# A Conformer encoder in float32r on one core: one weights tile with two offsets, casts in program order, and x sums moved by 96 bytes

## The chip, the cores and the metric

One NeuronCore of a Trainium2 chip runs the whole program. The metric is the device time of one execution in microseconds (us); lower is better. Before the change it is 1783.02 us, the median of 3 runs (1781.78 to 1783.49). Engines are named as in the profile: PE (TensorE), PEld (its weight loads), DVE (VectorE), ACT (ScalarE), POOL (GpSimd), SP (SyncE, which issues most loads).

## The reference

Two layers over 512 tokens of width 1024, with feed-forward width 2816:

```python
for l in range(DEPTH):                                   # 2
    x = x + 0.5 * swiglu(rms_norm(x, g1), gate1, up1, down1)
    p = rms_norm(x, gm) @ w_in                           # q and kv latents, rotary key, conv input
    x = x + concat(attention(p), conv(p)) @ w_out        # 8 heads, chunk mask; depthwise conv of 31 taps
    x = x + 0.5 * swiglu(rms_norm(x, g2), gate2, up2, down2)
    x = rms_norm(x, gp)
def swiglu(x, w_gate, w_up, w_down):
    return (silu(x @ w_gate) * (x @ w_up)) @ w_down
```

## The kernel before

x stays in the core's memory, features on partitions and tokens along the free axis. Every large product is made of float32r pieces: an operand is split into a high part `hi` (a cast to float32r on ACT) and a low part `lo = src - hi` (a subtraction on DVE), and `mm3` issues three matmuls on PE, hi by hi (L172), hi by lo (L173) and lo by hi (L174). The right-hand operand is the moving one, the weights the stationary one.

Four kinds of products fill PE:

- **Plain products**, 512 tokens at a time: `group` and `plain` call `mm3` with weights from `load_w`. This is all of the mixing stage (mix), the first two of eleven column pairs of each feed-forward net (FFN), and the last three pairs' down product. In `latent_k`, `queries` and `up_kv` the weights move and the activations are stationary, 288, 384 or 512 columns wide.
- **Strassen products** (`pair` and `down`), 256 columns at a time, called "b11", "t2", "t1", "b22" and so on: `product` issues 2 halves x 4 blocks x 3 = 24 matmuls from `split_into` weights. In the "b22" product half of the moving operands are the `xs` tiles and half are ring tiles; in the others all are ring tiles (`r`).
- **Joined products** ("b21", "t3", "t4"; `product_joined`, L391 and L392): 8 times a 512-column matmul on an `xj` tile (256 tokens of hi beside 256 of lo) and then a 256-column one. The low weights of "b21" and "t4" are in `ls` tiles.
- Attention, in float32, on ring tiles, `q`, `kn` and `m` tiles.

Weights arrive by SP in `raw` or `fr` tiles. `load_w` (L150), `split_into` (L262, L264) and `summed` (L415) take the next of four `wh` buffers for hi and of four `wl` buffers for lo. The scheduler orders the instructions of each engine; `issue_after` fixes some of them by hand.

Where the tiles start within a partition, in bytes modulo 1024, follows from the sizes of what is allocated ahead of them (and from three gaps: `gap`, `gap0`, `gap1`):

| tile | before | after |
|---|---|---|
| ring `r` | 704 | 704 |
| `wh` / `wl` of `load_w` (plain products) | 768 / 896 | 704 / 704 |
| `wh` / `wl` of `split_into`, `summed` (Strassen, joined) | 768 / 896 | 768 / 896 |
| `xs` (x sums of products that are not joined) | 800 | 704 |
| `xj`, `ls`, `fr`, `e`, `u` | 800 | 800 |
| `m`, `y`, `q`, `kn`, `pr` of the mixing stage | 800 | 704 |

A 128-column block of weights is 512 bytes, so a stationary operand starts at its tile's place or 512 bytes on.

Of the kernel before, what the change touches and what calls it, by code (L numbers as in the profile page):

```python
# [7 lines left out]
FP = mybir.dt.float32  # L8
FR = mybir.dt.float32r
# [3 lines left out]
ALU = mybir.AluOpType  # L13
AX = mybir.AxisListType

P = 128
D = 1024
S = 512
# [13 lines left out]
NF = F // P  # L32
EPS = 1e-6
WC = 1024
GAP = 96
HS = S // 2
RING = 35
WIDE = 6
# [11 lines left out]
POOLW = "wo"  # L50
# [29 lines left out]
def encoder_kernel(ctx: ExitStack, tc: tile.TileContext, xT, consts, vecs, rgain, wgu1, wd1, wdq1,  # L80
# [6 lines left out]
    wpool = ctx.enter_context(tc.tile_pool(name="w", bufs=4))  # L87
# [4 lines left out]
    def nm(s):  # L92
        uid[0] += 1
        return f"{s}{uid[0]}"
# [21 lines left out]

    small.tile([P, GAP], FP, tag="gap", name="gap", bufs=1)
    V, A, G, T = nc.vector, nc.scalar, nc.gpsimd, nc.tensor
# [30 lines left out]
    def load_w(src, w, kind=""):  # L149
        raw = wpool.tile([P, WC], FP, tag="raw", name=nm("raw"), bufs=3)  # L150
        nc.sync.dma_start(out=raw[:, :w], in_=src)
        hi = wpool.tile([P, WC], FR, tag="wh", name=nm("wh"))
        order["cast"] = A.copy(hi[:, :w], raw[:, :w]).ins  # L153
        lo = low()
        if kind == "sum":
            A.activation(lo[:, :w], raw[:, :w], AF.Copy, scale=-1.0)
            G.dma_start(out=lo[:, :w], in_=src, accum_op=ALU.add)
            return hi, lo
        (G if kind in POOLW.split() else V).tensor_tensor(lo[:, :w], raw[:, :w], hi[:, :w].bitcast(FP),  # L159
                                                          ALU.subtract)  # L160
        return hi, lo

    def low():
        return wpool.tile([P, WC], FR, tag="wl", name=nm("wl"))

    order = {}

# [82 lines left out]
    def groups(srcs, rhs, ws=None):  # L250

        ws = ws or [load_w(src, WC) for src in srcs]
        os = [bank() for _ in srcs]
        for ks in (range(KD - 1), range(KD - 1, KD)):
            for o, w in zip(os, ws):
                group(o, w, rhs, ks, KD)
        return os

    def split_into(q, src, w=WC):

        hi = wpool.tile([P, WC], FR, tag="wh", name=nm("wh"))
        A.copy(hi[:, :w], src[:, :w])  # L262
        lo = low()
        order["lo"] = V.tensor_tensor(lo[:, :w], src[:, :w], hi[:, :w].bitcast(FP), ALU.subtract).ins  # L264
        return hi, lo

    def ffn(l, gx, norm, wgu, wd, wdq, gain, done, w0=None, halved=KD):
# [3 lines left out]
    def ffn_body(fpool, l, gx, norm, wgu, wd, wdq, gain, done, w0, halved):  # L271
# [2 lines left out]

        def quarter():
            return fpool.tile([P, WC], FP, tag="fr", name=nm("fr"), bufs=4)
# [124 lines left out]
        def subtracted(w, src, n=WC):  # L404

            lo = fpool.tile([P, WC], FR, tag="ls", name=nm("ls"), bufs=2)
            A.activation(lo[:, :n], src[:, :n], AF.Copy, scale=-1.0)  # L407
            G.dma_start(out=lo[:, :n], in_=w, accum_op=ALU.add)  # L408
            return lo

        def summed(w, src, n=WC, lo=None):

            lo = subtracted(w, src, n) if lo is None else lo
            hi = wpool.tile([P, WC], FR, tag="wh", name=nm("wh"))
            A.copy(hi[:, :n], src[:, :n])  # L415
            return hi, lo

        def pair(p, quartered):

            a11, a12, a21, a22, s3 = quarters(wgu[l, p], WC, p == CHUNKS[0][1])  # L420
            bx, by, bz = bank(), (bank(), bank()), (bank(), bank())
            product(bx, split_into("a11", a11), "b11", True, True)
            a = copied(tmp(), bx)
            product_joined(by, summed(wgu[l, p, 1], a12), "b21", True)
            with after("first"):
                V.tensor_tensor(s3, a11, a21, ALU.add)
# [4 lines left out]
            for c, main, rest in parts(by):  # L431
                V.tensor_tensor(a[:, c], a[:, c], main, ALU.add)
                V.tensor_tensor(a[:, c], a[:, c], rest, ALU.add)
                if c.start == 0:
                    A.activation(s[:, 0:HS], a[:, 0:HS], AF.Silu)
            V.tensor_tensor(s[:, 0:HS], s[:, 0:HS], a[:, HS:S], ALU.mult)
            product(bx, split_into("s2", a11), "t2", False, True)
            r2 = wide(fpool.tile([P, WC], FP, tag="e", name=nm("e"), bufs=1))
            copied(r2[:, 0], bx)
            product_joined(bz, split_into("s3", s3), "t3", True)  # L440
            d = [copied(tmp(), o) for o in bz]
            for t in d:
# [3 lines left out]
            for t, (c, _, _) in zip(d, parts(bz)):  # L446
                order["first"] = V.tensor_tensor(r2[:, 1, c], t[:, 0:HS], r2[:, 1, c], ALU.subtract).ins
            product_joined(bz, summed(wgu[l, p, 3], a22), "t4", False)
            for c, main, rest in parts(bz):
                V.tensor_tensor(r2[:, 0, c], main, r2[:, 0, c], ALU.subtract)  # L450
# [28 lines left out]
        def down(act, chunk):  # L479

            n = 2 * NP * P
            for g in range(2):
# [3 lines left out]
                def times(o, src, name, start, q=None, lo=None):  # L486
                    hi, lo = split_into(name, src, n) if q is None else summed(wdq[l, g, chunk, q], src, n, lo)
                    with tc.issue_after(order["pe"]):
                        for k in range(NP):
                            for i in range(2):  # L490
                                c = slice((i * NP + k) * P, (i * NP + k + 1) * P)
                                last = mm3(o[:, i * HS:(i + 1) * HS], hi[:, c], lo[:, c], *act[k][name],
                                           start and k == 0 and i == 0, k == NP - 1, True)
                    order["pe"] = last
# [45 lines left out]
        for p0, p1 in CHUNKS:  # L540
# [3 lines left out]
            for p in range(p0, p1):  # L544
                if p == 0:
                    os = []
                    for r in range(2):
                        ws = w0[2 * r:2 * r + 2] if w0 else [load_w(wgu[l, p, 2 * r + q], WC) for q in range(2)]
                        os.append([bank(), bank()])
                        if w0 and not r:  # L550
                            plain_first(os[r], ws)
                        elif w0:
                            plain(os[r][:1], ws, range(KD))
                            plain([None] + os[r][1:], ws, range(KD // 2))
                            with tc.issue_after(order["mm"]):
                                norm()
                            with after("sums"):
                                plain([None] + os[r][1:], ws, range(KD // 2, KD))
                        else:
                            plain(os[r], ws, range(KD - 1))  # L560
                            plain(os[r], ws, range(KD - 1, KD))
                            if not w0:
                                R = norm()
                    if not w0:
                        scaled(os, R)
                elif p < CHUNKS[0][1]:
                    for r in range(2):
                        ws = [load_w(wgu[l, p, 2 * r + q], WC) for q in range(2)]
                        o = [bank(), bank()]
                        if w0 and not r:  # L570
                            with tc.issue_after(order["mm"]):
                                plain(o[:1], ws, KS[:KD // 4])
                            with tc.issue_after(order["mm"]):
                                R = norm()
                            with after("spread"):
                                plain(o[:1], ws, KS[KD // 4:])
                                plain([None] + o[1:], ws, range(KD))
                            scaled(os, R)
                        else:
                            plain(o, ws, range(KD))  # L580
                        advance(8)
                        act.append(plain_out(o, R))
                else:
                    order.setdefault("pe", order["mm"])
                    act += pair(p, p0 > 0 and not last)
# [9 lines left out]
            for m in range(halved if last else KD):  # L595
                if m in ahead:
                    pd, w = ahead[m]
# [440 lines left out]
    class Finish:  # L1038
# [37 lines left out]
        def part(self, h, src, first):  # L1076
            for t in range(2):
                i = T.matmul(self.ss[:, 2 * h + t:2 * h + t + 1], src[:, t * P:(t + 1) * P], ones[:, 0:1],
                             start=first and h == 0 and t == 0, stop=not first, skip_group_check=True)
            return i.ins  # L1080
# [26 lines left out]
    st = Stats()  # L1107
    f = gained(0, "g1", gx, first_gain)
    f(0)
    w0 = [tuple(wpool.tile([P, w], t, tag=tag, name=nm(tag), bufs=n) for t, tag, n, w in (  # L1110
        (FP, "raw", 3, WC), (FP, "gap0", 1, 16), (FR, "wh", 4, WC), (FP, "gap1", 1, 32), (FR, "wl", 4, WC)))[::2]
        for _ in range(2)]

    def half_w(q, gu):
        raw, hi, lo = (v[:, gu * 512:(gu + 1) * 512] for v in w0[q])
        nc.sync.dma_start(out=raw, in_=wgu1[0, 0, q, :, gu * 512:(gu + 1) * 512])
        A.copy(hi, raw)  # L1117
        V.tensor_tensor(lo, raw, hi.bitcast(FP), ALU.subtract)
    for m in KS:
        if m:  # L1120
            nc.sync.dma_start(out=x[:, m, :], in_=xT[m])
# [6 lines left out]
    w0 = [w[1:] for w in w0]  # L1128
# [172 lines left out]
```

## Time and profile before

| | |
|---|---|
| time, median of 3 runs | 1783.02 us |
| the profiled execution's own time | 1781.53 us |
| its span, first to last instruction | 1779.8 us |
| PE busy | 1768.6 us, 99% of the span |
| PEld / DVE / ACT / POOL busy | 88% / 83% / 62% / 22% |
| mean granted TensorE clock | 0.999 |

Matmuls overlap in the pipeline, so a matmul's own duration is longer than the time from its start to the next one's start. That time, here called the spacing, is what a stream of matmuls costs. It is read from windows of the trace: the length of a stretch without stalls, divided by the matmuls that start in it. Numbers of the trace are counted from the start of the span.

### The profile page before, as it was taken

What the parts mean: (1) busy time and instruction counts of PE and PEld (TensorE: products, weight loads), DVE (VectorE), ACT (ScalarE), POOL (GpSimd) and SP (SyncE); (2) the same over time, 40 slices, a digit from 0 to 9 for tenths busy, and PEclk for the clock granted to TensorE, in tenths of its full rate; (3) what the DMA queues carried; (4) which work ended last, traced back from release to release, by engine and by line L of the source; (5) the groups of instructions that cost most, each with busy time, mean ns of one, the idle gap of its engine ahead of it and who ended that gap; (6) DMA issues with size and microseconds to landing.
All of it is one profiled execution on the core that took longest, in us unless ns stands there. A gap on an engine that the chain in (4) does not pass through costs nothing.

```text
span 1779.8 us, 29441 instructions
## 1 busy us (share of the span) xinstructions
PE 1768.6 (99%) x11430; PEld 1558.0 (88%) x11430; DVE 1486.0 (83%) x2309; ACT 1094.9 (62%) x1699; POOL 383.3 (22%) x315
## 2 busy tenths in 40 slices
PE   9999999999999999999999999999999999999998
PEld 7899999888678899999888999998976788999997
DVE  7998988588965989998779989876989559999883
ACT  5576766456953575757645757554768435757664
POOL 1000000247822000000310000002576410000002
PEclk9999999999999999999999999999999999999999
DMA  5657574324203466665426575743260125575742
GB/s 170 165 140 186 136 189 114 109 86 124 71 25 101 124 162 162 159 166 131 123 66 167 125 197 124 198 112 112 80 157 24 58 68 155 150 180 140 186 117 74
DMA packets 71947, 228.28 MB, mean 128 GB/s; under 512 B 8448, under 2 KB 9600, under 8 KB 71808
## 3 DMA queue, kind: packets, MB, share of 16 engines
q1 hardware_dynamic: 55536, 171.87, 30.5%
q0 software_dynamic: 16128, 54.53, 18.3%
q8 instruction: 89, 1.46, 0.3%
q14 instruction: 50, 0.41, 0.1%
q10 hardware_dynamic: 144, 0.00, 0.0%
HBM read 222.19 MB, written 2.10 MB: 126 GB/s over the span
## 4 chain that ended last, share of the span: by engine, by line
PE 91%; DVE 5%; ACT 2%; issue 1%; DMA 1%; SPq 0%; ACTq 0%; DVEq 0%
PE ps L172 24%; PE ps L174 24%; PE ps L173 23%; PE ps L391 11%; PE ps L392 6%; DVE cv L972 1%; PE ps L921 1%; DVE mx L880 1%; PE ps L899 1%; DVE wl L264 1%; PE ps L876 0%; PE ps L678 0%; PE ps L216 0%; PE ps L914 0%; DVE r L902 0%
## 5 line engine op out<-in xcount | busy, mean ns | idle before, releaser
L172 PE MATMUL ps<-r,wh 128*128 128x256 f32 (+1 forms) x2556 | 808.8, 320 | 1.7 <-ACT wh L1117 0.6
L173 PE MATMUL ps<-r,wh 128*128 128x256 f32 (+1 forms) x2556 | 807.4, 316 | 0.8 <-DVE r L180 0.4
L174 PE MATMUL ps<-r,wl 128*128 128x256 f32 (+1 forms) x2364 | 753.9, 321 | 0.0
L172 PEld LDWEIGHTS ps<-r,wh 128*128 128x128 f32 x2556 | 480.6, 188 | 51.0 <-issue 3.7
L173 PEld LDWEIGHTS ps<-r,wh 128*128 128x128 f32 x2556 | 480.1, 188 | 42.7 <-DVE r L180 2.5
L174 PEld LDWEIGHTS ps<-r,wl 128*128 128x128 f32 x2364 | 444.1, 188 | 38.5 <-DVE wl L159 0.7
L391 PE MATMUL ps<-xj,wh 128*128 128x512 f32 x864 | 302.5, 390 | 0.0
L153 ACT CAST wh<-raw 128x1024 fp32r<-128x1024 f32 (+3 forms) x148 | 132.4, 900 | 227.9 <-PE ps L173 140.3
L262 ACT CAST wh<-fr 128x1024 fp32r<-128x1024 f32 (+1 forms) x160 | 157.8, 986 | 103.5 <-DVE fr L428 53.2
L159 DVE TENSOR_TENSOR wl<-raw,wh 128x1024 fp32r<-128x1024 f32 (+3 forms) x132 | 142.6, 1089 | 92.5 <-ACT wh L153 91.7
L408 POOL DMA_DIRECT2D ls<-in_wgu x72 | 62.5, 868 | 724.3 <-ACT ls L407 522.5
L264 DVE TENSOR_TENSOR wl<-fr,wh 128x1024 fp32r<-128x1024 f32 (+1 forms) x160 | 182.8, 1143 | 20.2 <-ACT wh L262 20.2
L391 PEld LDWEIGHTS ps<-xj,wh 128*128 128x128 f32 x864 | 160.8, 188 | 29.1
L392 PE MATMUL ps<-xj,ls 128*128 128x256 f32 x576 | 161.3, 280 | 0.0
L978 POOL TENSOR_TENSOR y<-y,pr 128x495 f32<-128x495 f32 (+29 forms) x90 | 120.3, 1339 | 46.6 <-ACT pr L976 41.2
L262 ACT CAST wh<-raw 128x1024 fp32r<-128x1024 f32 (+1 forms) x100 | 97.9, 979 | 42.1 <-PE ps L173 21.1
L264 DVE TENSOR_TENSOR wl<-raw,wh 128x1024 fp32r<-128x1024 f32 (+1 forms) x100 | 113.8, 1138 | 11.8 <-ACT wh L262 11.2
L392 PEld LDWEIGHTS ps<-xj,ls 128*128 128x128 f32 x576 | 108.1, 188 | 0.0
L209 POOL TENSOR_TENSOR r<-r,t 128x512 f32<-128x512 f32 x45 | 75.3, 1681 | 133.3 <-ACT t L205 132.7
L407 ACT ACTIVATE ls<-fr 128x1024 fp32r<-128x1024 f32 (+1 forms) x56 | 56.1, 1001 | 73.3 <-PE ps L392 41.5
L972 DVE SCALAR_TENSOR_TENSOR cv<-m,vec,cv 128x511 f32<-128x511 f32 (+14 forms) x120 | 88.1, 734 | 4.6 <-ACT cv L968 3.0
L408 POOL DMA_DIRECT2D ls<-in_wdq x32 | 27.6, 863 | 258.6 <-ACT ls L407 258.6
(258 smaller groups left out, 2921.5 us busy)
## 6 DMA issues: line engine op xcount, KB each, us to landing
fr<-in_wgu SPq DMA_DIRECT2D x112, 512.0 KB, 4.2
ls<-in_wgu POOLq DMA_DIRECT2D x72, 512.0 KB, 6.6
raw<-in_wgu SPq DMA_DIRECT2D x62, 512.0 KB, 4.6
fr<-in_wdq SPq DMA_DIRECT2D x48, 384.0 KB, 4.7
ls<-in_wdq POOLq DMA_DIRECT2D x32, 384.0 KB, 4.9
raw<-in_wd SPq DMA_DIRECT2D x32, 384.0 KB, 3.2
raw<-in_wd SPq DMA_DIRECT2D x32, 256.0 KB, 2.8
raw<-in_wcv SPq DMA_DIRECT2D x16, 512.0 KB, 3.6
```

What stands on the lines that cost most here:

```text
L153: order["cast"] = A.copy(hi[:, :w], raw[:, :w]).ins
L159: (G if kind in POOLW.split() else V).tensor_tensor(lo[:, :w], raw[:, :w], hi[:, :w].bitcast(FP), ALU.subtract)
L172: T.matmul(o, lh, rh, start=first, stop=False, skip_group_check=free)
L173: T.matmul(o, lh, rl, start=False, stop=False, skip_group_check=free)
L174: order["mm"] = T.matmul(o, ll, rh, start=False, stop=last, skip_group_check=free).ins
L262: A.copy(hi[:, :w], src[:, :w])
L264: order["lo"] = V.tensor_tensor(lo[:, :w], src[:, :w], hi[:, :w].bitcast(FP), ALU.subtract).ins
L391: T.matmul(o, w[0][:, c], both, start=start and k == 0, stop=False, skip_group_check=True)
L392: last = T.matmul(o[:, 0:HS], w[1][:, c], both[:, 0:HS], start=False, stop=k == 3, skip_group_check=True).ins
L408: G.dma_start(out=lo[:, :n], in_=w, accum_op=ALU.add)
L972: V.scalar_tensor_tensor(acc[:, s:], u[c][:, :S - s], tap(k), acc[:, s:], ALU.mult, ALU.add)
L978: order["conv"] = G.tensor_tensor(ys[c][:, s:], ys[c][:, s:], pr[:, s:], ALU.add).ins
```

## The change

The eight weight buffers become one tile, `weights`, of 2 x 4 parts of 1024 elements and 48 elements more. `part(j)` hands out hi parts (j = 0) and lo parts (j = 1) in turn. With `moved` the part starts 16 elements (64 bytes, hi) or 48 elements (192 bytes, lo) further on; `split_into` and `summed` use this, `load_w` does not. A moved part reaches into the next one, so going from moved to unmoved a part is left out. `in_turn` holds the casts, and the subtractions on one engine, in the order in which the program is written. The pool of an FFN takes two `xs` tiles and a gap of 96 bytes ahead of its other tiles; the `small` pool's gap is 96 bytes less.

```diff
-GAP = 96
+GAP = 72
+WN = 4
+WOFF = 16, 48
...
-        hi = wpool.tile([P, WC], FR, tag="wh", name=nm("wh"))
-        order["cast"] = A.copy(hi[:, :w], raw[:, :w]).ins
+        hi = part(0)
+        order["cast"] = in_turn("h", lambda: A.copy(hi[:, :w], raw[:, :w]))
...
+    weights = wpool.tile([P, 2 * WN * WC + WOFF[1]], FR, name="weights", bufs=1)
+    used, was = [0, 0], [False, False]
+    def part(j, moved=False):
+        if was[j] and not moved:
+            used[j] += 1
+        was[j] = moved
+        i = (j * WN + used[j] % WN) * WC + (WOFF[j] if moved else 0)
+        used[j] += 1
+        return weights[:, i:i + WC]
+    turns = {}
+    def in_turn(key, make):
+        with tc.issue_after(turns[key]) if key in turns else nullcontext():
+            turns[key] = make().ins
+        return turns[key]
...
     def split_into(q, src, w=WC):
-        hi = wpool.tile([P, WC], FR, tag="wh", name=nm("wh"))
-        A.copy(hi[:, :w], src[:, :w])
-        lo = low()
+        hi = part(0, True)
+        in_turn("h", lambda: A.copy(hi[:, :w], src[:, :w]))
+        lo = low(True)
...
+        fpool.tile([P, S], FR, tag="xs", name=nm("xs"), bufs=2)
+        fpool.tile([P, 24], FP, tag="gap", name=nm("gap"), bufs=1)
...
-    w0 = [tuple(wpool.tile([P, w], t, tag=tag, name=nm(tag), bufs=n) for t, tag, n, w in (
-        (FP, "raw", 3, WC), (FP, "gap0", 1, 16), (FR, "wh", 4, WC), (FP, "gap1", 1, 32), (FR, "wl", 4, WC)))[::2]
-        for _ in range(2)]
+    w0 = [(wpool.tile([P, WC], FP, tag="raw", name=nm("raw"), bufs=3), part(0), part(1)) for _ in range(2)]
```

The order of the instructions changes at few places. One stands in each FFN where the Strassen products end and the last pairs' down products begin. On PE, before (`ps_3368` is the last joined product's sum, `ps_3584` the first down group's, `ps_3364` that of "b22"):

```order
L391 MATMUL ps_3368<-xj_701,wh_3521 128x512
L392 MATMUL ps_3368<-xj_701,ls_3518 128x256
L172 MATMUL ps_3584<-r_3118,wh_3587 128x512
L173 MATMUL ps_3584<-r_3119,wh_3587 128x512
L174 MATMUL ps_3584<-r_3118,wl_3589 128x512
L172 MATMUL ps_3584<-r_3122,wh_3587 128x512
L173 MATMUL ps_3584<-r_3123,wh_3587 128x512
L174 MATMUL ps_3584<-r_3122,wl_3589 128x512
```

After, on PE at the same place (`ps_3395` is the down group's sum, `ps_3187` that of "b22"; L194 to L196 are the former L172 to L174, and L416 and L417 the former L391 and L392):

```order
L416 MATMUL ps_3191<-xj_670,weights 128x512
L417 MATMUL ps_3191<-xj_670,ls_3332 128x256
L194 MATMUL ps_3395<-r_2953,weights 128x512
L195 MATMUL ps_3395<-r_2954,weights 128x512
L194 MATMUL ps_3187<-r_498,weights 128x256
L195 MATMUL ps_3187<-r_499,weights 128x256
L196 MATMUL ps_3187<-r_498,weights 128x256
L194 MATMUL ps_3187<-r_498,weights 128x256
```

The 24 matmuls of the last "b22" product have moved ahead, from behind eleven matmuls of the down group to behind two. On ACT at the same place, before (the casts of `raw` are those of the down weights):

```order
L401 COPY t_3481<-ps_3367 128x512
L153 CAST wh_3587<-raw_3585 128x768
L401 COPY t_3483<-ps_3368 128x512
L153 CAST wh_3619<-raw_3617 128x768
L401 COPY e_3459<-ps_3364 128x512
L153 CAST wh_3652<-raw_3650 128x768
L454 ACTIVATE t_3543<-e_3459 128x512
L153 CAST wh_3685<-raw_3683 128x768
```

And after, on ACT:

```order
L426 COPY t_3297<-ps_3190 128x512
L426 COPY t_3299<-ps_3191 128x512
L155 CAST weights<-raw_3396 128x768
L426 COPY e_3277<-ps_3187 128x512
L155 CAST weights<-raw_3426 128x768
L479 ACTIVATE t_3356<-e_3277 128x512
L155 CAST weights<-raw_3457 128x768
L155 CAST weights<-raw_3488 128x768
```

The first three of these casts stand behind one more operation each; the fourth follows the third directly. Of all 11071 PE instructions 382 change their place, the farthest by 24; the instructions themselves are the same.

More of the change, by code (lines that the diff above doesn't have):

```diff
@@ L158, in load_w, with low @@
             return hi, lo
-        (G if kind in POOLW.split() else V).tensor_tensor(lo[:, :w], raw[:, :w], hi[:, :w].bitcast(FP),
-                                                          ALU.subtract)
+        e = G if kind in POOLW.split() else V
+        in_turn(e, lambda: e.tensor_tensor(lo[:, :w], raw[:, :w], hi[:, :w].bitcast(FP), ALU.subtract))
         return hi, lo
-    def low():
-        return wpool.tile([P, WC], FR, tag="wl", name=nm("wl"))
+    weights = wpool.tile([P, 2 * WN * WC + WOFF[1]], FR, name="weights", bufs=1)
[12 more added lines that the diff above has]
+        return turns[key]
+    def low(moved=False):
+        return part(1, moved)
     order = {}
@@ L259, in split_into @@
     def split_into(q, src, w=WC):
-        hi = wpool.tile([P, WC], FR, tag="wh", name=nm("wh"))
-        A.copy(hi[:, :w], src[:, :w])
-        lo = low()
-        order["lo"] = V.tensor_tensor(lo[:, :w], src[:, :w], hi[:, :w].bitcast(FP), ALU.subtract).ins
+        hi = part(0, True)
+        in_turn("h", lambda: A.copy(hi[:, :w], src[:, :w]))
+        lo = low(True)
+        order["lo"] = in_turn(V, lambda: V.tensor_tensor(lo[:, :w], src[:, :w], hi[:, :w].bitcast(FP), ALU.subtract))
         return hi, lo
@@ L413, in summed @@
             lo = subtracted(w, src, n) if lo is None else lo
-            hi = wpool.tile([P, WC], FR, tag="wh", name=nm("wh"))
-            A.copy(hi[:, :n], src[:, :n])
+            hi = part(0, True)
+            in_turn("h", lambda: A.copy(hi[:, :n], src[:, :n]))
             return hi, lo
@@ L1116, in half_w @@
         nc.sync.dma_start(out=raw, in_=wgu1[0, 0, q, :, gu * 512:(gu + 1) * 512])
-        A.copy(hi, raw)
-        V.tensor_tensor(lo, raw, hi.bitcast(FP), ALU.subtract)
+        in_turn("h", lambda: A.copy(hi, raw))
+        in_turn(V, lambda: V.tensor_tensor(lo, raw, hi.bitcast(FP), ALU.subtract))
     for m in KS:
```

## The prediction

> **What bounds the kernel now.** I read the page first: busy times, the granted clock, the chain that ended last. Then I read what PE waited for.
>
> ```profile
> PE 1768.6 (99%) x11430; PEld 1558.0 (88%) x11430; DVE 1486.0 (83%) x2309; ACT 1094.9 (62%) x1699; POOL 383.3 (22%) x315
> PEclk9999999999999999999999999999999999999999
> PE 91%; DVE 5%; ACT 2%; issue 1%; DMA 1%; SPq 0%; ACTq 0%; DVEq 0%
> ...
> PE ps L133 <- DVE ones L129: 1.1, 1, 1.1
> PE ps L876 <- ACT r L884: 1.0, 2, 0.5
> PE ps L172 <- ACT wh L1117: 0.6, 1, 0.6
> PE ps L173 <- DVE r L180: 0.4, 1, 0.4
> ```
>
> PE is busy for 99% of the span at full clock, is 91% of the chain, and the four rows of its waits sum to 3.1 us. So the time is the number of matmuls times their spacing, and the change leaves the number as it is. Only a change of spacing, or a new wait on PE, can move the end. The spacing differs between products of one shape, as these windows of PE show (window, us, PE busy with the count of instructions, clock, DMA share, GB/s):
>
> ```profile
> 91.69:94.53 2.84, 2.84 (x26) 1.00 0.01 3
> 94.53:97.29 2.76, 2.76 (x26) 1.00 0.89 140
> 97.29:100.05 2.76, 2.76 (x19) 1.00 0.29 56
> 313.20:355.14 41.94, 41.94 (x182) 1.00 0.35 107
> ```
>
> The first two are a "b22" and the "t1" product behind it: both have 24 matmuls of 256 columns (the counts of 26 take in neighbours that reach into the window). "b22", half of it on `xs`, takes 2.84 us, or 118.3 ns each; the all-ring one takes 2.76, or 115.0. The timeline inside that one shows what it settles to:
>
> ```profile
> 95.59 0.28 PE L172 MATMUL ps<-r,wh 128*128 128x256 f32 x1
> ...
> 96.95 0.28 PE L172 MATMUL ps<-r,wh 128*128 128x256 f32 x1
> ```
>
> Twelve matmuls start between the two, 1.36 us, so the settled spacing is 113.3 ns. The same shape at the same clock costs 118.3 or 113.3; what differs is where the moving operand starts (800 against 704). So the place of the operands has a price, about 5 ns in 256 columns. The DMA share is no cause: it is 0.01 in the slower window and 0.89 in the faster.
>
> The fourth window is plain 512-column work; its groups are
>
> ```profile
> L174 PE MATMUL ps<-r,wl 128*128 128x512 f32 x61 | 24.0, 396 | 0.0
> L173 PE MATMUL ps<-r,wh 128*128 128x512 f32 x60 | 23.4, 392 | 0.0
> L172 PE MATMUL ps<-r,wh 128*128 128x512 f32 x60 | 23.1, 393 | 0.0
> ```
>
> 181 matmuls in 41.94 us: 231.7 ns each. Two settled 256-column matmuls cover as many columns in 226.6. So plain products pay about 5 ns over the best that this trace has, with weights at 64 and 192 bytes from the ring's place.
>
> **The change part by part.**
>
> *xs to the ring's place.* The rows of `xs`:
>
> ```profile
> L172 PE MATMUL ps<-xs,wh x144: 277/281/283, 92.4 to 1737.1; 128*128 128x256 f32 x144
> ```
>
> A "b22" has four such matmuls, so there are 144 / 4 = 36 such products. Afterwards each has the operands of "t1" as to place: 36 x (2.84 - 2.76) = 2.9 us less. If all 24 matmuls come at 113.3 (2.72 us), it is 36 x 0.12 = 4.3 us. I take 2.9, the whole product's row; below nothing is unlikely, since the ring's place is the one that all other 256-column products use.
>
> *Plain weights to the ring's place.* How many matmuls this concerns:
>
> ```profile
> L174 PE MATMUL ps<-r,wl 128*128 128x512 f32 x852 | 334.0, 396 | 0.0
> L173 PE MATMUL ps<-r,wh 128*128 128x512 f32 x852 | 333.4, 392 | 0.0
> L172 PE MATMUL ps<-r,wh 128*128 128x512 f32 x852 | 331.3, 399 | 0.7 <-ACT wh L1117 0.6
> ...
> L172 PE MATMUL ps<-wh,r 128*128 128x512 f32 x32 | 12.7, 398 | 0.0
> ...
> L172 PE MATMUL ps<-m,wh 128*128 128x512 f32 x16 | 6.5, 406 | 0.0
> ```
>
> With three lines each: 3 x (852 + 32 + 16) = 2700 matmuls of 512 columns, some 626 us at 231.7 ns. Moving and stationary operand now start at the same place modulo 512. No plain product of the trace shows this. The nearest row is the joined product with `ls`, where both stand at 800: the third window has 8 pairs in 2.76 us, 345 ns a pair. The pair's 256-column half also moves from 800, as in "b22"; at 118.3 ns it leaves 226.7 for the 512-column half. This equals twice 113.3. I take it: 2700 x (231.7 - 226.7) = 13.5 us less. The lower end of the spacing: if the joined half also pays the 5 ns of a start at 800, a start at 704 gives 221.7, and 27 us less. The upper end is above 231.7, since equal places are untried here for this pattern: by the dearest difference that the rows show, 5 ns per 256 columns, up to 241.7 and 27 us more.
>
> The Trainium skill, "TensorE: Matmul & The Clock Gate", Back-to-back issue gap, gives N / 2.4 + 2.5 ns for warm matmuls; 512 columns would come to an estimated 215.8 ns, and 2700 of them would save 43 us. No window here comes near it in float32r: the best 256-column row, 113.3, stands above its 109.2 as well, so the trace decides and the sum does not use it.
>
> The 288- and 384-column products of the mixing stage (192 and 144 by the groups) get the same new place. At 5 ns each they would give 336 x 5 = 1.7 us in either direction; I take nothing. Attention's `m` tiles move from 800 to 704: L921 is 1% of the chain, 18 us, and 5 in 113 of it is 0.8 us either way; nothing again.
>
> ```profile
> PE ps L172 24%; PE ps L174 24%; PE ps L173 23%; PE ps L391 11%; PE ps L392 6%; DVE cv L972 1%; PE ps L921 1%; DVE mx L880 1%; PE ps L899 1%; DVE wl L264 1%; PE ps L876 0%; PE ps L678 0%; PE ps L216 0%; PE ps L914 0%; DVE r L902 0%
> ```
>
> *Casts in turn, one tile.* Moved and unmoved parts overlap by 64 or 192 bytes, so where the kinds meet a cast can wait for a part read later than its own. The place with least room is the end of the Strassen products, four times in the program. There the first down cast now stands behind one more COPY. Before:
>
> ```profile
> 302.36 0.83 ACT L153 CAST wh<-raw 128x768 fp32r<-128x768 f32 x1 [0.44 <-PE ps L391]
> 303.10 0.58 ACT L401 COPY t<-ps 128x512 f32<-128x512 f32 x1
> ...
> 307.80 0.40 PE L172 MATMUL ps<-r,wh 128*128 128x512 f32 x1
> ```
>
> The cast ends at 303.19 and PE first reads it at 307.80: 4.6 us of room. Behind the COPY (ends 303.68) it would end near 304.5, and waiting for most of a 24-matmul product more (up to 2.8 us) near 306; DVE's subtraction and the next COPY queue behind it. PE keeps 1.8 us or more, so nothing reaches the end. With the cover gone it would be up to 2.8 us four times, 11 us. Elsewhere ACT waits for PE and not PE for ACT, as the waits above show. "b22" going ahead of nine down matmuls on PE is work changing places, worth nothing.
>
> *Sum.* 2.9 + 13.5 = 16.4 us less. The profiled execution took 1781.5 us (span 1779.8 and 1.7 around it), so 1765.1. It stands 1.5 us below the median of 1783.0; against the median the forecast is 1766.6 us.
>
> **The rivals.**
>
> *Equal places collide (slower).* The two reads of a plain product start at one place, and a moving read that shares its place with the next weight load may be held up through the whole row. Its price is the trace's bad place: 5 ns (one hold-up for each matmul) to 10 ns (one per 256 columns) over 231.7. That is 13.5 to 27 us more, less the 2.9 of `xs`: 1794 to 1807. It decides as soon as the plain spacing is over 231.7 + 2.9 / 2.7 = 232.8 ns. Against it: the joined window has equal places and no dear half. For it: the joined half is followed by a different shape, and starts at 800.
>
> *Only xs gains.* The plain spacing depends on the pattern of three 512-column matmuls, not on the place, and stays at 231.7. Then 2.9 to 4.3 us go: 1778.7 to 1780.1. The Trainium skill, "TensorE: Matmul & The Clock Gate", Step-by-step, says that PE has two independent read ports and that loading the next weights takes no read bandwidth from the running matmul. By that rule place would matter nowhere and the time would stay at 1783. The 2.84 against 2.76 us above speaks against the rule in general, not in the plain products, where no run so far varies the place.
>
> *The new order costs.* The cover at the four meeting points fails, and the plain products gain nothing: 11 - 2.9 = 8 us more, 1791. The 4.6 us of room speak against it.
>
> **How the numbers follow.** Forecast 0.57, with a range of its own from 1752 (221.7 ns and 4.3 us) to 1773 (half of the 13.5); collision 0.21; only xs 0.17; order 0.05. The range 1750 to 1792 holds the forecast, "only xs", the order and the mildest collision, and leaves out most of the collision's span, under 2 in 10. A measurement here can tell about 0.2%, 3.6 us, from no change. "Only xs" ends on both sides of that bound: I give 0.05 of it to faster, 0.12 to the same. So faster 0.62, same 0.12, slower 0.26.
>
> **What would show it.** In the trace after: a plain stretch near 226.7 ns a matmul (right), at 231.7 (only xs) or over 232.8 (collision); a "b22" window of 2.72 to 2.76 us; joined pairs still 345 ns; PE's waits still about 3 us. The forecast is wrong if the plain spacing does not fall, or if PE gains a row of waits for ACT's casts.

## The result and the profile after

The changed kernel takes 1775.37 us (median of 6 runs, 1773.71 to 1775.86) against 1782.56 us for the kernel before on the same chip: ratio 0.9957, 95% interval 0.9945 to 0.997. That is 7.2 us less, where 16.4 us were forecast. The profiled execution took 1773.71 us, with a span of 1771.9 us at a mean granted clock of 0.999.

The windows of PE in the trace after, at the places that the prediction showed of before: a "b22", the "t1" behind it, the joined product behind that, and a stretch of plain 512-column work (window, us, busy times with counts of PE, PEld, DVE, ACT and POOL, clock, DMA share, GB/s):

```profile
92.41:95.17 2.76, 2.76 (x26) 2.76 (x25) 2.76 (x4) 1.69 (x2) 0.86 (x1) 1.00 0.00 1
95.17:97.89 2.72, 2.72 (x26) 2.72 (x25) 2.72 (x6) 1.52 (x3) 0.00 (x0) 1.00 0.97 143
97.89:100.76 2.87, 2.87 (x18) 2.34 (x16) 2.87 (x5) 2.84 (x5) 0.00 (x0) 1.00 0.27 53
313.81:354.85 41.04, 41.04 (x182) 33.97 (x181) 25.40 (x30) 18.50 (x27) 9.50 (x6) 1.00 0.39 119
```

The plain stretch has 181 matmuls in 41.04 us, 226.7 ns each (before 231.7). "b22" fell from 2.84 to 2.76 us, and "t1" from 2.76 to 2.72. Both gains are there, to the digit. But the joined window grew from 2.76 to 2.87 us, and PE's waits have a new list, double in sum (engine, tile and line that waits, what for: us in all, times, longest):

```profile
PE ps L196 <- DVE weights L162: 2.3, 3, 0.9
PE ps L901 <- ACT r L909: 1.5, 3, 0.5
PE ps L135 <- DVE ones L131: 1.1, 1, 1.1
PE ps L194 <- ACT weights L155: 0.4, 1, 0.4
PE ps L882 <- DVE r L927: 0.4, 1, 0.4
PE ps L194 <- ACT weights L1140: 0.3, 1, 0.3
PE ps L196 <- DVE weights L286: 0.3, 1, 0.3
```

They sum to 6.3 us, against 3.1 before. The largest row is new: the subtraction of plain weights on DVE. One more wait is not in this list: it holds a weight load, and PE loses only about 0.1 us by it each time. The groups of weight loads (PEld; after the bar: busy, mean ns, idle and what ended it) show it:

```profile
L194 PEld LDWEIGHTS ps<-r,weights 128*128 128x128 f32 x2556 | 480.2, 188 | 50.8 <-ACT t L426 6.3 <-issue 3.7 <-DVE x L523 2.3
```

Before, this copy (there L401) was not among the first three of the row:

```profile
L172 PEld LDWEIGHTS ps<-r,wh 128*128 128x128 f32 x2556 | 480.6, 188 | 51.0 <-issue 3.7 <-DVE x L498 2.4 <-ACT wh L153 2.1
```

L426 copies the "b11" sum out of its PSUM bank, and "t2" writes to that bank next. So the first weight load of "t2" must wait for the copy, and the copy stands on ACT behind casts. The timeline at one such place, before:

```profile
98.89 0.62 ACT L179 CAST r<-t 128x512 fp32r<-128x512 f32 x1
99.41 0.58 ACT L401 COPY t<-ps 128x512 f32<-128x512 f32 x1
...
99.71 0.19 PEld L392 LDWEIGHTS ps<-xj,ls 128*128 128x128 f32 x1
...
100.05 0.19 PEld L172 LDWEIGHTS ps<-r,wh 128*128 128x128 f32 x1
100.05 0.39 PE L172 MATMUL ps<-r,wh 128*128 128x256 f32 x1
...
100.27 0.28 PE L173 MATMUL ps<-r,wh 128*128 128x256 f32 x1
```

And after:

```profile
99.61 0.62 ACT L201 CAST r<-t 128x512 fp32r<-128x512 f32 x1
100.13 0.58 ACT L426 COPY t<-ps 128x512 f32<-128x512 f32 x1
...
100.31 0.19 PEld L417 LDWEIGHTS ps<-xj,ls 128*128 128x128 f32 x1
...
100.76 0.19 PEld L194 LDWEIGHTS ps<-r,weights 128*128 128x128 f32 x1 [0.26 <-ACT t L426]
...
100.99 0.28 PE L195 MATMUL ps<-r,weights 128*128 128x256 f32 x1
```

Before, the copy ended at 99.99 and the weight load of "t2" started at 100.05; after, it is 100.71 and 100.76. The load follows the copy within 0.06 us both times, so it waited for the copy before the change as well. Its idle time was then 0.15 us (from 99.90, where the load ahead of it ended, to 100.05). The views name only longer waits, and so it stands in no list; a load that waits for nothing has 0.04 us here, as "copy first" below shows. PE paid for it too: the first matmul of "t2" starts 0.22 us ahead of the second, where "copy first" has 0.12. Over the 24 places where this is so, the load's idle time is 0.142 to 0.151 us before and 0.256 to 0.267 after.

So at these places the copy on ACT set the pace already. A PE that comes earlier only waits longer: the 0.11 us by which the joined window grew (2.87 - 2.76). The row's 6.3 us at 0.26 us each make 24 places, and 24 x 0.11 is 2.6 us of PE's time.

The whole balance, from the distance of each matmul's start to the next, summed by shape in both traces (what is far over the shape's usual distance counted as waits): plain 512-column matmuls -12.7 us of spacing and +3.4 of waits; 256 columns -3.1 of spacing and +1.3 of waits; joined products +2.7, the wait for the copy; float32 matmuls +0.8; 288 and 384 columns -0.2. That is -7.8 us, and the span fell by 7.9.

### The profile page after: what moved, and what is told of

The parts are those of the page before. It is cut to its first block, busy times and chain, and to the rows that moved or that the text cites. A ratio compares the mean times of both kernels' runs of the same rounds, so it can differ in the third digit from the quotient of the medians.

```text
span 1771.9 us, 29449 instructions
## 1 busy us (share of the span) xinstructions
PE 1757.3 (99%) x11430; PEld 1556.4 (88%) x11430; DVE 1488.5 (84%) x2309; ACT 1096.3 (62%) x1699; POOL 381.8 (22%) x315
## 5 line engine op out<-in xcount | busy, mean ns | idle before, releaser
L194 PE MATMUL ps<-r,weights 128*128 128x256 f32 (+1 forms) x2556 | 805.2, 318 | 1.8 <-ACT weights L155 0.4
L195 PE MATMUL ps<-r,weights 128*128 128x256 f32 (+1 forms) x2556 | 805.6, 315 | 0.7
L196 PE MATMUL ps<-r,weights 128*128 128x256 f32 (+1 forms) x2364 | 749.6, 318 | 2.9 <-DVE weights L162 2.3
L194 PEld LDWEIGHTS ps<-r,weights 128*128 128x128 f32 x2556 | 480.2, 188 | 50.8 <-ACT t L426 6.3
L195 PEld LDWEIGHTS ps<-r,weights 128*128 128x128 f32 x2556 | 480.5, 188 | 37.3 <-DVE r L202 2.4
L196 PEld LDWEIGHTS ps<-r,weights 128*128 128x128 f32 x2364 | 444.2, 188 | 38.5 <-DVE weights L162 3.6
L416 PE MATMUL ps<-xj,weights 128*128 128x512 f32 x864 | 302.5, 390 | 0.0
L155 ACT CAST weights<-raw 128x1024 fp32r<-128x1024 f32 (+3 forms) x148 | 131.7, 902 | 213.7 <-PE ps L195 120.4
L284 ACT CAST weights<-fr 128x1024 fp32r<-128x1024 f32 (+1 forms) x160 | 157.8, 986 | 99.7 <-DVE fr L453 49.4
L162 DVE TENSOR_TENSOR weights<-raw,weights 128x1024 fp32r<-128x1024 f32 (+3 forms) x132 | 142.9, 1091 | 81.5 <-ACT weights L155 80.3
L286 DVE TENSOR_TENSOR weights<-fr,weights 128x1024 fp32r<-128x1024 f32 (+1 forms) x160 | 182.3, 1140 | 20.7 <-ACT weights L284 20.7
L416 PEld LDWEIGHTS ps<-xj,weights 128*128 128x128 f32 x864 | 160.8, 188 | 29.1
L417 PE MATMUL ps<-xj,ls 128*128 128x256 f32 x576 | 161.3, 280 | 0.0
L284 ACT CAST weights<-raw 128x1024 fp32r<-128x1024 f32 (+1 forms) x100 | 98.0, 980 | 44.5 <-PE ps L195 23.5
L286 DVE TENSOR_TENSOR weights<-raw,weights 128x1024 fp32r<-128x1024 f32 (+1 forms) x100 | 113.5, 1135 | 11.5 <-ACT weights L284 10.9
L417 PEld LDWEIGHTS ps<-xj,ls 128*128 128x128 f32 x576 | 108.1, 188 | 0.0
```

The source lines that it names most:

```text
L155: order["cast"] = in_turn("h", lambda: A.copy(hi[:, :w], raw[:, :w]))
L162: in_turn(e, lambda: e.tensor_tensor(lo[:, :w], raw[:, :w], hi[:, :w].bitcast(FP), ALU.subtract))
L194: T.matmul(o, lh, rh, start=first, stop=False, skip_group_check=free)
L195: T.matmul(o, lh, rl, start=False, stop=False, skip_group_check=free)
L196: order["mm"] = T.matmul(o, ll, rh, start=False, stop=last, skip_group_check=free).ins
L284: in_turn("h", lambda: A.copy(hi[:, :w], src[:, :w]))
```

## The experiments

Theory: both place effects are as forecast, some 16 us together, and half of it comes back because PE now meets the work of ACT and DVE that had just kept ahead of it. Rival: the spacings gain less than the windows show, or the casts held in turn are what costs.

**xs alone.** The kernel before, with this one part of the change:

```diff
-GAP = 96
+GAP = 72
...
+        fpool.tile([P, S], FR, tag="xs", name=nm("xs"), bufs=2)
+        fpool.tile([P, 24], FP, tag="gap", name=nm("gap"), bufs=1)
```

> The kernel before with the xs tiles alone moved to the ring's place (800 to 704); weights stay at 768 and 896. My theory (the b22 products get faster, and the next pair gives it back because PE then waits for ACT's copy of the b11 sum out of PSUM): a b22 product of 2.72 to 2.76 us in place of 2.84, joined products behind it longer by about 0.1 us, and the time unchanged within 1 us: 1782 to 1783. Rival (the gain counts in full, as the prediction had it): 2.9 to 4.3 us less, 1778 to 1780.

Measured: 1782.49 us, ratio 0.9998 [0.9989, 1.0006]: nothing that can be told from zero. The row of weight loads says why:

```profile
L172 PEld LDWEIGHTS ps<-r,wh 128*128 128x128 f32 x2556 | 480.3, 188 | 54.2 <-ACT t L403 6.3 <-issue 3.7 <-ACT wh L153 2.5
```

It has the same 6.3 us behind the copy as the changed kernel. By the distances of starts, 256-column spacing fell by 2.9 us, and joined products took 2.7 and 256-column waits 1.3 us more.

**Weights alone.** The changed kernel without the `xs` part:

```diff
-GAP = 72
+GAP = 96
...
-        fpool.tile([P, S], FR, tag="xs", name=nm("xs"), bufs=2)
-        fpool.tile([P, 24], FP, tag="gap", name=nm("gap"), bufs=1)
```

> The changed kernel without the move of xs: plain weights at the ring's place, one tile, casts in turn. My theory: all of the measured gain is here, 1775 to 1776, with plain products at 226.7 to 227 ns. Rival (xs brings its 2.9 us): 1778 to 1779.

Measured: 1776.93 us, ratio 0.9957 [0.9944, 0.9971], the same ratio as the whole change. So in the change as made the `xs` part brings nothing measurable, and the weights' part alone gives the 7 us; each of the two ratios is uncertain by some 2 us.

**No turns.** The changed kernel, with casts and subtractions free to go in the order that the scheduler likes:

```diff
-        with tc.issue_after(turns[key]) if key in turns else nullcontext():
+        with nullcontext():
```

> The changed kernel with the same tile and places, but with the casts and subtractions no longer held in program order; the scheduler alone places them. If the fixed order is what makes PE wait in the plain down products of the first pairs (about 3.4 us given back there): 1772 to 1773, and PE's waits for DVE's subtraction at L162 gone. If PE waits because it arrives earlier at a DVE that is busy throughout: 1775 to 1776, as the changed kernel.

Measured: 1786.78 us, ratio 1.0017 [1.0008, 1.0026]. PE's waits:

```profile
PE ps L195 <- DVE r L202: 3.5, 8, 0.7
PE ps L196 <- DVE weights L286: 3.1, 9, 0.7
PE ps L196 <- DVE weights L162: 2.3, 3, 0.9
```

The turns don't cause the 2.3 us at L162, since these stay without them. But without them the changed kernel is 11 us slower and no gain at all. That they are needed because the parts of the one tile overlap is likely; no run here separates it.

**Tile and turns alone.** The changed kernel with every part and `xs` put back at the old places:

```diff
     def part(j, moved=False):
+        moved = True
...
-GAP = 72
+GAP = 96
...
-        fpool.tile([P, S], FR, tag="xs", name=nm("xs"), bufs=2)
-        fpool.tile([P, 24], FP, tag="gap", name=nm("gap"), bufs=1)
```

> One tile and casts in turn, with all operands at the places of the kernel before (weights at 768 and 896 for every product, xs at 800). It prices the tile and the order alone. If the order costs: 1784 to 1786, with PE waits for casts near 63 us and 607 us. If it costs nothing by itself: 1782 to 1783. Plain products at 231.7 ns either way.

Measured: 1784.97 us, ratio 1.0006 [0.9998, 1.0015]. The plain spacing stays at 231.7 ns, and one new wait appears:

```profile
PE ps L197 <- DVE weights L162: 1.7, 3, 0.9
```

So most of the wait at L162 comes with the one tile, with the turns or without them, and even at the old spacing. What the three traces with the one tile have in common (the changed kernel, "no turns" and this one) is the order on ACT there: the last cast of `r` stands behind an ACTIVATE of `ls`, which waits 1.2 to 1.4 us for a transfer, and DVE then waits 0.3 to 0.45 us for that cast, ahead of the subtraction at L162. In the kernel before, the cast stood ahead of the ACTIVATE. By the time, tile and turns cost 1.1 us, with an interval from 0.4 less to 2.7 more, which doesn't exclude nothing.

**Equal places for all.** The kernel before with the two gaps of the weight buffers taken out, so that weights of 512 and of 256 columns alike start at the ring's place:

```diff
-GAP = 96
+GAP = 144
...
-        (FP, "raw", 3, WC), (FP, "gap0", 1, 16), (FR, "wh", 4, WC), (FP, "gap1", 1, 32), (FR, "wl", 4, WC)))[::2]
+        (FP, "raw", 3, WC), (FR, "wh", 4, WC), (FR, "wl", 4, WC)))
```

> The kernel before with its eight separate weight buffers, its order and its xs place, but without the two gaps of 64 and 128 bytes between the pools, so that all weights, those of the 256-column products too, start at the ring's place modulo 512 (the small pool's gap grows by 192 bytes, so that nothing else moves). Plain products 226.7 ns, so 12.7 us less there, and none of the 2.2 us of waits that the one tile brought. Theory A, that 256-column products settle at 113.3 at an equal place too: 1769 to 1771. Theory B, that 256 columns want other places than 512 (the reason for two offsets): 118 to 119 ns on some 5300 matmuls, part of it hidden where DVE sets the pace: 1785 to 1797.

Measured: 1794.29 us, ratio 1.0058 [1.0045, 1.007]. The windows of "b22" and "t1":

```profile
91.98:94.85 2.87, 2.87 (x27) 2.87 (x25) 2.87 (x5) 1.69 (x2) 0.86 (x1) 1.00 0.08 23
94.85:97.72 2.87, 2.87 (x27) 2.87 (x25) 2.87 (x5) 1.80 (x3) 0.00 (x0) 1.00 0.95 156
```

24 matmuls in 2.87 us are 119.6 ns, where "t1" had 115.0 before and has 113.3 after. The 512-column spacing is good here too (12.1 us less by the starts); the 256-column work pays 22 us, the joined products 4 of them. For the products on ring tiles an equal place is right for 512 columns and wrong for 256: this is why the kernel needs two offsets in one tile.

**Plain weights 128 bytes off.** The changed kernel, with

```diff
-        i = (j * WN + used[j] % WN) * WC + (WOFF[j] if moved else 0)
+        i = (j * WN + used[j] % WN) * WC + (WOFF[j] if moved else 32)
```

> The changed kernel with plain weights 128 bytes from the ring's place in place of 0. If what counts is the exact equality of the places: plain products back at 231.7 ns, 1787 to 1789. If it is the distance modulo 128 bytes (64 and 192 were dear, 0 cheap): 226.7 ns and 1775 to 1776.

Measured: 1786.27 us, ratio 1.0016 [1.0007, 1.0025]. The plain stretch:

```profile
314.64:356.48 41.84, 41.84 (x181) 33.92 (x180) 25.16 (x29) 18.46 (x27) 9.55 (x6) 1.00 0.37 117
```

180 to 181 matmuls in 41.84 us are 231 to 232 ns. The whole 512-column gain is gone; of the places tried for plain products (0, 64, 128 and 192 bytes from the moving operand's), only equality gives 226.7.

**Copy first.** The changed kernel; the copy of the "b11" sum is put ahead of the next casts on ACT:

```diff
-            a = copied(tmp(), bx)
+            a = tmp()
+            order["b11"] = A.copy(a, bx).ins
...
-            product_joined(bz, split_into("s3", s3), "t3", True)
+            with after("b11"):
+                ws3 = split_into("s3", s3)
+            product_joined(bz, ws3, "t3", True)
```

> The changed kernel with ACT's copy of the b11 sum out of PSUM ahead of the casts for the t3 and t1 products (those casts are held behind the copy). My theory, that this copy is what gives back the gain of xs: PE's wait at the end of 24 joined products goes, 24 x 0.107 = 2.6 us, 1772.5 to 1773.5. Rival: DVE, busy for 91% and more of the Strassen stage, sets the pace, and another wait (the subtraction for t2 or t3) takes its place: 1775 to 1776.

Measured: 1769.94 us, ratio 0.9924 [0.9911, 0.9936]. At the place shown above, ACT, PE and PEld now have

```profile
98.33 0.58 ACT L449 COPY t<-ps 128x512 f32<-128x512 f32 x1
...
100.41 0.19 PEld L417 LDWEIGHTS ps<-xj,ls 128*128 128x128 f32 x1
...
100.64 0.28 PE L417 MATMUL ps<-xj,ls 128*128 128x256 f32 x1
100.64 0.19 PEld L194 LDWEIGHTS ps<-r,weights 128*128 128x128 f32 x1
...
100.75 0.28 PE L194 MATMUL ps<-r,weights 128*128 128x256 f32 x1
...
100.87 0.28 PE L195 MATMUL ps<-r,weights 128*128 128x256 f32 x1
```

and the weight loads have lost that wait:

```profile
L194 PEld LDWEIGHTS ps<-r,weights 128*128 128x128 f32 x2556 | 480.4, 188 | 45.5 <-issue 3.7 <-DVE x L526 2.3 <-ACT weights L155 1.4
```

The span is 1768.2, 3.7 us below the changed kernel's: 2.5 us in the joined products and 1.6 in the waits of 256-column work, less small losses elsewhere. The second part is the 0.1 us that the copy had cost the first matmul of each "t2" before the change as well: at all 24 places that matmul now takes 0.12 us to the next one's start in place of 0.22, and at 8 of them PE stops once for 0.1 us a few matmuls later. By the ratios the gain over the changed kernel is near 6 us, uncertain by 3; by the trace it is half as much again as expected, in the expected place.

**The copy without the places, and with xs only.** The same edit in the kernel before, and in the kernel of "xs alone":

> The kernel before with only the earlier copy of the b11 sum on ACT; all places and the order of casts otherwise as they were. Theory: before the change the copy ended just ahead of PE's need (0.06 us), so PE did not wait for it and nothing is to be gained: 1782.5 to 1784 us, ratio 0.9995 to 1.0005. Rival: the earlier copy is worth more than the waits that the trace names (the changed kernel gained 5.5 us by it, where 24 waits of 0.107 us make 2.6); then about 3 us show here too: 1780 to 1781 us.

> The kernel before with xs at the ring's place (which alone gave 1782.5 us, ratio 0.9998) and the earlier copy of the b11 sum. Theory: the 36 b22 products are 3.1 us faster by the spacing, and what took it back was the wait for that copy; with the copy out of the way the 3 us reach the end: 1780 to 1781 us, ratio 0.998 to 0.9985. Rival: another engine (DVE, busy 30.4 of 32 us there) sets the end of these stretches; then 1782.5 to 1783.5 us.

Measured: copy only 1781.69 us, ratio 0.9992 [0.9984, 1.0001]; with `xs` 1778.49 us, ratio 0.9978 [0.9968, 0.9987]. Alone the copy is worth nothing that can be told from zero, near what the theory said, but the theory's reason doesn't hold. PE did wait, and the earlier copy removes it: at all 24 places the first matmul of "t2" takes 0.12 us in place of 0.22, 2.5 us in all. Most of this doesn't last: the matmuls behind it start 115.2 ns apart on the mean, where they had 113.5 after the hold-up, 1 us in all, and at 8 places PE stops once in "t2", by which the product is 0.13 us longer. With `xs` moved as well the ratio is 0.9978, where `xs` alone had 0.9998 and the copy alone 0.9992. Some 3 us below the kernel before were expected; the interval holds 2.3 to 5.7. What `xs` adds to the copy is near 2.5 us, and the two intervals overlap; the spans of the two profiled executions (1779.8 and 1778.2) differ by 1.6.

**All FFN tiles at the ring's place.** The changed kernel without the gap behind `xs`, so that `xj`, `ls` and the FFN's other tiles start at 704 as well:

```diff
-        fpool.tile([P, 24], FP, tag="gap", name=nm("gap"), bufs=1)
```

> The changed kernel with all tiles of the FFN's pool (xj, ls, fr, e, u) at the ring's place, not xs alone. Joined pairs on ls would fall from 345 to 340 ns, and the down products on ls from 119 to 113.3, about 7 us of PE time. My theory, that the Strassen stage is paced by DVE and ACT: 1774.5 to 1776, unchanged. Rival, PE sets the pace there: 1768 to 1770. If 256 columns are dear at an equal place: joined pairs at 345 or more.

Measured: 1771.95 us, ratio 0.9933 [0.9919, 0.9946], between the two expectations. With `xj` at 704 the 256-column half of a joined pair with `ls` takes 113 to 114 ns instead of 118, by the starts, although `xj` and `ls` still start at one place; so "dear at an equal place" doesn't hold here. The down products on `ls` gained less than expected: 117 to 118 ns instead of 118 to 120. And part of the gain went again to the copy of the "b11" sum:

```profile
L194 PEld LDWEIGHTS ps<-r,weights 128*128 128x128 f32 x2556 | 479.9, 188 | 53.8 <-ACT t L425 8.4 <-issue 3.7 <-DVE x L522 2.3
```

That is 8.4 us where the changed kernel has 6.3; by the starts, the joined products gained 2.5 us of spacing and waited 2.2 us longer.

**Both.** Copy first and all FFN tiles at the ring's place:

> The changed kernel with both edits that gained: the copy of the b11 sum ahead of two casts on ACT (1769.9 us alone), and all of the FFN's operand tiles at the ring's place (1772.0 us alone, 3 to 4 us below the changed kernel at its 1775.4). Theory: the two act at different places, the one on a wait of PE, the other on the spacing of 256-column matmuls that read xj with ls, so they add up: 1765.5 to 1767 us, ratio near 0.990, with the 256-column half of joined pairs at 113 to 114 ns and no waits at the start of t2. Rival: the second edit gained only because it moved PE away from the same wait; then the sum is that of the copy alone, 1769 to 1770.5 us.

Measured: 1765.61 us (1764.97 to 1766.42), ratio 0.9904 [0.9889, 0.992]: the best version, 17 us below the kernel before. A window of seven joined pairs:

```profile
97.81:100.19 2.38, 2.38 (x17) 2.10 (x15) 2.38 (x4) 2.38 (x4) 0.00 (x0) 1.00 0.35 69
```

2.38 / 7 = 340 ns a pair, which is 226.7 and 113.3. The two edits add up, as the theory had it. What is left of the waits is the other half:

```profile
PE ps L196 <- DVE weights L162: 2.4, 3, 0.9
```

**Residual additions later.** The kernel of "copy first"; in the plain down product that opens each FFN's pairs, four additions on DVE go behind the subtraction for which PE waits:

```diff
...
-                order["evicted"] = V.scalar_tensor_tensor(x[:, m, :], pd, 0.5, x[:, m, :], ALU.mult, ALU.add).ins
+                due.append((m, pd))
+                if p0 == 0 and m in range(4):
+                    continue
+                for i, (q, o) in enumerate(due):
+                    with tc.issue_after(turns[V]) if p0 == 0 else nullcontext():
+                        order["evicted"] = V.scalar_tensor_tensor(x[:, q, :], o, 0.5, x[:, q, :], ALU.mult, ALU.add).ins
+                due.clear()
```

> The changed kernel with the earlier copy, and in the plain down product at the start of each FFN's pairs the first four residual additions put behind the subtraction of the fifth weights on DVE. Theory: PE's three waits for that subtraction (2.3 us in the trace) come from what stands ahead of it on DVE, and go: 1767.5 to 1768.5 us against 1769.9 without this edit. Rival: DVE is full there, and the wait only moves to the next subtraction or to a freed bank: 1769.5 to 1770.5 us.

Measured: 1774.47 us, ratio 0.9948 [0.9936, 0.996], 4 us slower than without the edit: both theory and rival missed. The place in the changed kernel first, DVE and then PE:

```profile
62.46 0.69 DVE L362 TENSOR_TENSOR r<-t,r 128x512 fp32r<-128x512 f32 x1 [0.45 <-ACT r L361]
63.07 0.68 DVE L632 SCALAR_TENSOR_TENSOR x<-ps,x 128x512 f32<-128x512 f32 x1
63.67 0.68 DVE L354 TENSOR_TENSOR xj<-t,xj 128x512 fp32r<-128x512 f32 x1
64.27 1.28 DVE L632 SCALAR_TENSOR_TENSOR x<-ps,x 128x512 f32<-128x512 f32 x2
65.47 0.68 DVE L162 TENSOR_TENSOR weights<-raw,weights 128x512 fp32r<-128x512 f32 x1
...
66.20 0.50 PE L196 MATMUL ps<-r,weights 128*128 128x512 f32 x1 [0.91 <-DVE weights L162]
```

With the edit, DVE's subtraction is early and SP's next transfer goes out at once, but what comes next on ACT and PE is this:

```profile
63.88 0.68 DVE L162 TENSOR_TENSOR weights<-raw,weights 128x512 fp32r<-128x512 f32 x1
...
64.60 0.33 SPq L153 DMA_DIRECT2D raw<-in_wd  x1
...
71.29 0.62 ACT L155 CAST weights<-raw 128x512 fp32r<-128x512 f32 x1 [2.67 <-DMA raw<-in_wd]
...
71.96 0.50 PE L194 MATMUL ps<-r,weights 128*128 128x512 f32 x1 [1.79 <-ACT weights L155]
```

In "copy first" the same two are

```profile
66.26 0.33 SPq L153 DMA_DIRECT2D raw<-in_wd  x1
...
70.75 0.62 ACT L155 CAST weights<-raw 128x512 fp32r<-128x512 f32 x1 [2.09 <-DMA raw<-in_wd]
```

With the edit the transfer was issued 1.7 us earlier and its cast came 0.5 us later. The window of the 2 us in which it was issued (the last two columns are DMA share and GB/s), and PE's waits over the whole trace:

```profile
64.00:66.00 2.00, 2.00 (x9) 1.38 (x9) 2.00 (x4) 0.72 (x2) 0.00 (x0) 1.00 1.01 217
```

```profile
PE ps L194 <- ACT weights L155: 3.3, 4, 1.8
...
PE ps L196 <- DVE weights L162: 0.6, 1, 0.6
```

DVE's order is the cause of the wait at L162: it fell from 2.3 to 0.6 us. But behind it stands the transfer of the weights, and PE, now earlier, waits longer for that. By the distances of starts, plain products wait 3.8 us longer than in "copy first" and 256-column products 0.9, which is about the difference of the two spans (1772.7 and 1768.2). Why the earlier transfer took longer is not shown. The DMA engines are full in its first 2 us, but in "copy first" they are as full while the later and faster one runs (shares of 1.01 and 1.03 from 66 to 70 us).

## Why the prediction was right and wrong

*Plain weights to the ring's place: right in the number.* 226.7 ns was forecast and measured; 12.7 us by the starts against 13.5. The row that it was read from is another case than the prediction says, though. In a joined pair the `ls` tile at 800 holds the weights of the 256-column half; the 512-column half has its own in `wh`, at 768, and `xj` at 800. Its two operands are 32 bytes apart. Equal to `xj` is the place of the weights that are loaded while it runs. That 226.7 carried over to plain products was in part luck.

*xs: right in the spacing, wrong in the sum.* 2.9 us were forecast, 3.1 came on the 256-column matmuls, and 2.7 went at once to the copy of the "b11" sum. "xs alone" showed no gain. (The 5 ns of the prediction compare the mean of a whole "b22", 118.3, with the settled spacing inside "t1", 113.3; product against product it was 118.3 and 115.0, and the sum went by these.)

*Joined pairs, 288 and 384 columns: right.* Joined pairs still take 345 ns apart from the wait behind them (2.87 - 0.11 = 2.76 for eight), and the other widths moved by 0.2 us.

*Casts in turn, one tile: wrong place.* The end of the Strassen products, which was given 4.6 us of room, stayed without a large wait. But the plain down products that open an FFN's pairs, the first some 60 us into the trace, were not looked at, and there PE now waits for DVE: 2.3 us at L162, of which 1.7 come without any change of place. "No turns" has these waits too, so it is the one tile that brings them and not the turns.

*The step that failed* is the sum. It took all 16.4 us of spacing off the time, on the sentence that elsewhere ACT waits for PE and not PE for ACT "as the waits above show", and so put new waits at nothing. The spacing came, 16.0 us by the starts; 8.2 of them came back as waits and small losses. The list of PE's waits, 3.1 us in sum, could not show this. At 24 places the weight load of "t2" was already held by ACT's copy, each time for 0.15 us, which the views don't name; there a faster "b22" and "t1" bought only a longer wait, 2.7 us, and "copy first" gives it back. At the plain down products 3.4 us of waits came, most of them for DVE's subtraction. 1.3 us came in 256-column products, as in "xs alone", and 0.8 in float32 matmuls, which no run explains. The prediction had named a sign for this, PE's waits "still about 3 us": they rose to 6.3, and more for DVE than for ACT's casts, which it had feared.

*The rivals.* "Equal places collide" did not happen in 512 columns. It does happen in 256 on ring tiles, as "equal places for all" shows, slower by 0.58%. "Only xs gains" is the reverse of what happened. "The new order costs" holds in kind, at another place: 1.7 us of waits in the trace of "tile and turns alone", not 11, and by the time 1.1 us, which can't be told from nothing. The rule of the Trainium skill, "TensorE: Matmul & The Clock Gate", Step-by-step, on two independent read ports, by which place would not matter, does not agree with 226.7 against 231.7 ns for one shape at one clock.

## What to carry to other kernels

When PE is busy for 99% and a change makes it faster, look for each product at when its last input or its freed bank comes, and when PE starts with it. Where a matmul or a weight load starts right behind what released it (here 0.05 us), another engine sets the pace already, and time that PE gains ahead of that place is lost there. A list of waits need not show such a place: here the wait before the change was 0.15 us on a weight load and 0.1 us on PE, in no list, and 24 such places took back all that `xs` had gained. So look at the idle time of the weight loads as well, and compare it with that of a load that waits for nothing. In this kernel the earlier copy brought nothing measurable before the change, and 3.7 us by the trace after it.

## What the runs showed of the hardware

The start of moving and stationary operand modulo 512 bytes changes the spacing of float32r matmuls, and each width wants something else. For plain and Strassen products on ring tiles, by the distance between a matmul's two operands: 512 columns take 226.7 ns where both start at one place, and 231 to 232 at a distance of 64, 128 or 192 bytes. 256 columns settle at 113.3 ns at a distance of 64 or 192 bytes, and take 118 to 120 ns at none; on `xs` before, 32 and 96 bytes off, they took 118 to 120 too. 288 and 384 columns moved by less than 1% between the kernel before, the changed kernel and "equal places for all".

Joined pairs don't fit this count. In "all FFN tiles" the 256-column half of a pair with `ls` has both operands at 704 and takes 113 to 114 ns. The 512-column half has its weights 64 bytes off in every pair; it takes 226.6 ns on the mean in pairs with `ls`, and 231.3 in "t3" pairs, where the next weights are 192 bytes off. The trace has a weight load start together with the matmul ahead of it (100.64 in "copy first"), so the place of the weights that are loaded while a matmul runs may be what counts. The 256-column half of "t3" pairs, with 118 ns there, doesn't fit that either. Which of the two counts, and what makes it so, no run here tells.

An earlier DMA issue can land later: at one place, in one execution each, 256 KB of weights took 6.6 us from issue to landing where they were issued 1.7 us earlier, and 4.4 us in "copy first".
